# Seven of eight eighths of an MLP's down projection as seven products each, on one NeuronCore

## The chip, the cores and the metric

One core of a Trainium2 chip. The metric is device time in microseconds (us) of one launch. Times of instructions come from one execution that the hardware profiler recorded. PE is TensorE's matmuls, PEld its weight loads, DVE VectorE, ACT ScalarE, POOL GpSimd, SP the engine that issues most transfers.

## What is computed

Two layers of an encoder block on 512 tokens of width 1024, in f32: a mixer (attention and retention), an MLP, and a gated addition. The part that matters here:

```python
u = rms_norm(h, norm_mlp_pre[i])
ff = jnp.square(jax.nn.relu(u @ w_mlp_up[i])) @ w_mlp_down[i]
h = h + rms_norm(ff, norm_mlp_post[i])
gate = jax.nn.sigmoid(rms_norm(h) @ w_ple_gate[i])
h = h + gate * rms_norm(p[i] @ w_ple_proj[i], norm_ple[i])
```

`w_mlp_up` is 1024 x 4096, `w_mlp_down` 4096 x 1024, `w_ple_gate` 1024 x 1024.

## The kernel before, in words

**Matrix products.** Every f32 operand is split into a high part (rounded to fp32r, on ACT) and a low part (the rest, on DVE or POOL). A product of two operands is three matmuls, high x high, high x low and low x high (`HL`, L295). A matmul has a 128 x 128 stationary block and up to 512 moving columns.

**Weights.** They lie in DRAM in the order of use, `PLAN`, as chunks of 512 KB (128 x 1024). `prefetch` (L271) loads a chunk on SP's queue (L254) into one of 4 `raw` buffers, splits it on ACT (L278) and mostly DVE (L301, through `low`) into one of 5 `wt` buffers, up to three items ahead of the one that `chunk` (L289) hands to PE.

**The MLP.** The 4096 inner columns are 32 up chunks. `up_job(c)` (L879) multiplies one (24 matmuls), `evac_up` (L890) applies relu and square. The down projection is cut into eighths of 512 inner rows. The first six (`UNITS`, L56) are done by seven products in place of eight: of a 2 x 2 cut of an eighth (tokens in halves, rows in halves, output columns in halves) `operands` (L826) forms sums of activation blocks on DVE, in a chain in which each of x, y and v needs the one before; `total` (L260) forms the sums of weight blocks by transfers that POOL issues and that add into a buffer (L268); `product` (L843) multiplies (12 matmuls) and `evac_prod` (L855) adds the result to an accumulator `prod` in SBUF (L860). The accumulators of all eighths are folded into the four output quarters once, in the last group: seven additions of 128 x 1024 on DVE (L915), listed in `FOLD`.

The groups are interleaved with the up chunks of the next eighth: up, P1, P5, up, P7, P6, up, P3, P4, up, P2 (L906 to L914). `_slot` (L63) gives the same order to the weights in `PLAN`, and `_items` (L93) to what is converted.

**The plain part.** The last two eighths' activations are kept split (`ff`, L893 to L898); after four more up chunks, `row_job` (L332) runs them as plain products: for each half of the output columns, four weight chunks, 96 matmuls. In the first half each chunk goes over all four token tiles (t); in the second (`ONES`) one tile after another is completed. `h`, which waits in DRAM, is reloaded on SP before (L920) into buffers that the folds free.

**Behind it.** When a tile's second half is complete, `evac_dn` (L929) starts its chain: add to the accumulator (DVE, L933), mean square (ACT, L351), rstd (two small operations on POOL, L359 and L361), gain, residual (DVE, L926), mean square again (ACT), rstd (POOL), `un` (DVE, L403), a transpose of `un` on PE (L413) and the split of the result into `uT` (ACT L416, DVE L417). The gate's matmuls (`pg`) read `uT`. The first half's gain goes on POOL (L935). `un` has two buffers free at this point. A tile's transposes are put into PE's order `AGE_DN` = 6 steps after its end (a step is 6 matmuls in this part), or at the latest by `settle` (L389), in front of the first gate matmul that reads that tile; the gate begins with tiles 0 and 1.

**What sets the order.** PE's order is that of the program text (L206). The other engines' queues are laid out when the program is built, by priority among what is expected to be ready; each then runs in that order. `soon` (L375) raises the priority of an evacuation by 300.

Of the kernel before, what the change touches and what calls it, by code (L numbers as in the profile page):

```python
# [52 lines left out]
ROPE_POOL = ()  # L53
POOL_LOW = ("qa", "ka", "qr", "kr", "vr", "g", "ga", "ao")

UNITS = 6  # L56


def _dn(e, hf, k):
    return 8 * (e // 2) + 4 * hf + 2 * (e % 2) + k  # L60


def _slot(e):  # L63
    up = [("up", 4 * e + 4 + c) for c in range(4)]
    b11, b21, b12, b22 = (("dn", _dn(e, hf, k)) for hf in range(2) for k in range(2))
    return [up[0], b11, b12, up[1], b22, up[2], b21, up[3]]


# [13 lines left out]
    + [("pp", c) for c in range(2)]  # L82
    + [("up", c) for c in range(4)]
    + [x for e in range(UNITS) for x in _slot(e)]
    + [("up", c) for c in range(28, 32)]
    + [("dn", c) for c in range(24, 32)]
    + [("pg", c) for c in range(8)]
)
PLAN = [(i,) + x for i in range(NL) for x in PLAN_LAYER]
CHUNK = {x: n for n, x in enumerate(PLAN)}  # L90


def _items():  # L93
    out = []
    for i in range(NL):
        for kind, c in PLAN_LAYER:
            e = 2 * (c // 8) + c % 4 // 2
            if kind == "up" and c >= 4 and c // 4 <= UNITS:
                e, at = c // 4 - 1, c % 4
                b11, b21, b12, b22 = (CHUNK[i, "dn", _dn(e, hf, k)] for hf in range(2) for k in range(2))  # L100
                out.append(((i, "up", c), (CHUNK[i, "up", c],)))
                out += [((i, p, e), src) for p, src in (
                    (("P1", (b11,)), ("P5", (b11, b12))),
                    (("P7", (b12, b22)), ("P6", ("chain", b22))),
                    (("P3", (b22,)), ("P4", ("chain", b21))),
                    (("P2", (b21,)),),
                )[at]]
            elif kind != "dn" or e >= UNITS:
                out.append(((i, kind, c), (CHUNK[i, kind, c],)))
    return out  # L110


ITEMS = _items()
ITEM = {key: m for m, (key, _) in enumerate(ITEMS)}
LAST = {src[0]: m for m, (_, src) in enumerate(ITEMS) if len(src) == 1}
# [84 lines left out]
def block(ctx: ExitStack, tc: tile.TileContext, x, pT, w, dl, gains, cs, lc, rel, eye, out):  # L200
# [12 lines left out]
    def blk(tag, shape, dt=F32, name="blk"):  # L213
        return big.tile(shape, dt, name=name, tag=tag, bufs=NAMES[tag])
# [7 lines left out]
    def bank(tag):  # L222
        b = banks[tag].pop(0)
        banks[tag].append(b)
        return b
# [63 lines left out]
    def chunk(*key):  # L289
        m = ITEM[key]  # L290
        n = max(x for _, src in ITEMS[max(0, m - 3):m + 4] for x in src if x != "chain")
        prefetch(n + 3, m + 4)
        return wt[m]
# [13 lines left out]
    def t_job(key, ps, rhs=None, kts=KD, off=0):  # L307
        t = chunk(*key)
        for k in range(kts):
            for n, (a, b) in enumerate(HL):  # L310
                r = uT[:, b, k, :] if rhs is None else rhs[k][:, b, :]
                nc.tensor.matmul(ps, lhsT=t[:, a, (off + k) * P:(off + k + 1) * P], rhs=r,  # L312
                                 start=k == 0 and n == 0, stop=k == kts - 1 and n == 2)
            if k % 2:
                step()
# [4 lines left out]
    def row_mm(ps, ch, j, lhs, k, t, first, last):  # L320
        for n, (a, b) in enumerate(HL):
            nc.tensor.matmul(ps, lhsT=lhs(a, k, t), rhs=ch[:, b, j * S:(j + 1) * S],  # L322
                             start=first and n == 0, stop=last and n == 2)

    def step(age=None):
        clock[0] += 1
        age = AGE if age is None else age
        if pending and clock[0] - pending[0][0] >= age:
            soon(pending.pop(0)[1])()
        tick()  # L330

    def row_job(keys, lhs, evac, groups=ALL, age=None):  # L332
        n = len(keys)
        chs = {}
        for grp in groups:
            if lhs is u_lhs:
                settle(grp)
            pss = [bank(ROW_BANKS[n]) for n in range(len(grp))]
            for c in range(len(keys)):
                if grp is groups[0]:  # L340
                    chs[c] = chunk(*keys[c])
                for t, ps in zip(grp, pss):
                    for j in range(2):
                        row_mm(ps, chs[c], j, lhs, 2 * c + j, t, c == 0 and j == 0, c == n - 1 and j == 1)
                    if c == n - 1:
                        evac(t, ps)
                    step(age)
# [41 lines left out]
    def settle(ts):  # L389
        while any(t in unready for t in ts):  # L390
            soon(pending.pop(0)[1])()
# [247 lines left out]
    def one_layer(i, h):  # L639
# [113 lines left out]
        for c in range(8):  # L753
            src = fb[c // 2][:, c % 2, :]
# [44 lines left out]
        def ple_norm(t):  # L799
            junk = blk("R", [P, D], name="pjunk")  # L800
            r = rstd_of(sumsq(pn[t], junk, 4e-6, 1.0 / 16))
            nc.gpsimd.tensor_scalar(pn[t], pn[t], r, 1.0, op0=ALU.mult, op1=ALU.mult)
            nc.gpsimd.tensor_tensor(pn[t], pn[t], g_ple, op=ALU.mult)
# [22 lines left out]
        def operands(f1, f2):  # L826
            a11, a21, a12, a22 = f1[:, :, :256], f1[:, :, 256:], f2[:, :, :256], f2[:, :, 256:]
            ops = {}
            x, y, z, v = (t2(n).rearrange("p (s n) -> p s n", s=2) for n in ("sx", "sy", "sz", "sv"))
            operand(ops, "P1", a11)  # L830
            nc.vector.tensor_tensor(x, a22, a21, op=ALU.subtract)
            operand(ops, "P5", x)
            nc.vector.tensor_tensor(z, a11, a21, op=ALU.subtract)
            operand(ops, "P7", z)
            nc.vector.scalar_tensor_tensor(y, x, -1.0, a11, op0=ALU.mult, op1=ALU.subtract)
            operand(ops, "P6", y)
            nc.vector.scalar_tensor_tensor(v, y, -1.0, a12, op0=ALU.mult, op1=ALU.subtract)
            operand(ops, "P3", v)
            operand(ops, "P4", a22)
            operand(ops, "P2", a12)  # L840
            return ops

        def product(e, x, op):  # L843
            t = chunk(i, x, e)
            for j in range(2):
                ps = dn_bank()
                for k in range(2):
                    for n, (a, b) in enumerate(HL):
                        nc.tensor.matmul(ps, lhsT=op[:, a, k, j * P:(j + 1) * P], rhs=t[:, b, k * S:(k + 1) * S],  # L849
                                         start=k == 0 and n == 0, stop=k == 1 and n == 2)  # L850
                evac_prod(e, x, j, ps)
                step(AGE_DN)
# [26 lines left out]
        def up_job(c):  # L879
            if c < EARLY:  # L880
                ps = early[c]
            else:
                ps = bank("s")
                t_job((i, "up", c), ps)
            if 2 <= c < 6:
                ple_norm(c - 2)
            evac_up(c, ps)

        @soon
        def evac_up(c, ps):  # L890
            r = t2("relu")
            nc.scalar.activation(r, ps, AF.Relu)  # L892
            if c >= 4 * UNITS:  # L893
                b = blk("A", [P, 2, S], F32R, name="ff")
                nc.scalar.activation(b[:, 0, :], r, AF.Square)
                nc.vector.tensor_tensor(r, r, r, op=ALU.mult)
                nc.vector.tensor_tensor(b[:, 1, :], r, b[:, 0, :].bitcast(F32), op=ALU.subtract)
                half_f.append(b)  # L898
                return
            if c % 2 == 0:  # L900
                half_f.append(blk("P", [P, 2, S], name="f"))
            nc.scalar.activation(half_f[-1][:, c % 2, :], r, AF.Square)

        for c in range(4):
            up_job(c)
        for e in range(UNITS):  # L906
            ops = operands(*half_f)
            half_f = []
            for n, xs in enumerate((("P1", "P5"), ("P7", "P6"), ("P3", "P4"), ("P2",))):
                up_job(4 * e + 4 + n)  # L910
                for name in xs:
                    product(e, name, ops[name])
                    if e == UNITS - 1:
                        for to, of in FOLD.get(name, ()):  # L914
                            nc.vector.tensor_tensor(prod[to], prod[to], prod[of], op=ALU.add)  # L915
        for c in range(28, 32):
            up_job(c)
        for t in range(NT):
            h[t] = blk("V", [P, D], name="hr")
            nc.sync.dma_start(h[t], hm[t])  # L920
# [17 lines left out]
            return f  # L938

        for hf in range(2):  # L940
            row_job([(i, "dn", 24 + 4 * hf + c) for c in range(4)],
                    lambda a, k, t: half_f[k][:, a, t * P:(t + 1) * P], evac_dn(hf), ONES if hf else ALL, AGE_DN)

        if not last:
# [20 lines left out]
        if last:  # L965
            t, f = NT - 1, evac_pg(1)
            for j in range(CUTS):
                cut = slice(j * S // CUTS, (j + 1) * S // CUTS)
                n = cut.stop - cut.start
# [67 lines left out]
```

## Time and profile before

| | |
|---|---|
| three runs, median (lowest to highest) | 1794.32 us (1794.28 to 1795.28) |
| the profiled execution, and its span | 1794.64 us, 1792.9 us |
| PE busy | 1772.4 us, 99% of the span |
| DVE, ACT, POOL busy | 64%, 45%, 21% |
| MLP of layer 0, last group of products | 745 to 786 us |
| its four further up chunks | 786 to 808 us |
| its plain part | 808 to 854 us |

The span runs from the first to the last instruction; the execution's own time has some 1.7 us around it. "Busy" counts an engine from an instruction's start to its end, so waits inside the order of work are seen in the idle time that a row gives in brackets, with the instruction or transfer that ended it.

### The profile page before, as it was taken

The page shows a single profiled execution, that of the slowest core. Times are in us where ns is not written, and L with a number is a line of the kernel's source. Part 1 is how long each engine was busy: PE and PEld are TensorE (multiplying, and loading weights), DVE is VectorE, ACT ScalarE, POOL GpSimd, SP SyncE. Part 2 cuts the span into 40 slices and gives each one's busy share as a digit, 9 for nine tenths or more (in the row PEclk, how much of TensorE's full clock was granted, in tenths as well). Part 3 has the DMA queues.
Part 4 walks back from the last instruction along what each step waited for, and adds up shares of the span by engine and source line. Part 5 has one row for each costly group of instructions (what it writes and reads, how often), then busy time and mean ns, then how long its engine had stood idle before and what let it go on. Part 6 is the DMA issues. An engine that isn't in the chain of part 4 may idle for free.

```text
span 1792.9 us, 22127 instructions
## 1 busy us (share of the span) xinstructions
PE 1772.4 (99%) x8209; PEld 1466.2 (82%) x8209; DVE 1145.4 (64%) x1803; ACT 807.5 (45%) x1271; POOL 382.6 (21%) x354
## 2 busy tenths in 40 slices
PE   8999999999999999999999999999999999999998
PEld 6888788888898888888788887888888888888887
DVE  6676777743465677674656767677444657667754
ACT  4255444332466454433443555444333664444342
POOL 2312244311142001002123222442012410000030
PEclk9999999999999999999999999999999999999999
DMA  5555464552347655552346545555422566664421
GB/s 213 194 193 159 149 212 137 166 175 95 117 142 188 165 158 161 156 184 70 129 141 214 165 145 172 184 159 187 136 101 99 165 170 156 169 175 130 165 71 60
DMA packets 87807, 274.58 MB, mean 153 GB/s; under 512 B 11921, under 2 KB 20497, under 8 KB 87698
## 3 DMA queue, kind: packets, MB, share of 16 engines
q1 hardware_dynamic: 80786, 247.99, 40.7%
q0 software_dynamic: 6912, 25.17, 8.3%
q8 instruction: 65, 1.06, 0.2%
q14 instruction: 44, 0.36, 0.1%
HBM read 239.55 MB, written 33.55 MB: 152 GB/s over the span
## 4 chain that ended last, share of the span: by engine, by line
PE 89%; DVE 4%; POOL 2%; ACT 2%; issue 1%; DMA 1%; SPq 0%; POOLq 0%; ACTq 0%
PE acc L312 28%; PE acc L322 19%; PE s L312 18%; PE acc L849 8%; PE tp L849 4%; PE tp L612 2%; PE tp L544 2%; PE tp L507 2%; PE acc L871 1%; PE tp L413 1%; POOL wt L301 1%; PE s L525 1%; PE s L526 1%; PE s L590 1%; PE s L871 1%
## 5 line engine op out<-in xcount | busy, mean ns | idle before, releaser
L312 PE MATMUL acc<-uT,wt 128*128 128x512 f32 x1920 | 472.8, 392 | 0.0
L312 PEld LDWEIGHTS acc<-uT,wt 128*128 128x128 f32 x1920 | 356.2, 188 | 71.8
L301 DVE TENSOR_TENSOR wt<-raw,wt 128x1024 fp32r<-128x1024 f32 x217 | 279.4, 1292 | 187.6 <-ACT wt L278 187.1
L278 ACT ACTIVATE wt<-raw 128x1024 fp32r<-128x1024 f32 x280 | 293.9, 1055 | 223.0 <-PE acc L312 114.0
L322 PE MATMUL acc<-wt,uT 128*128 128x512 f32 x1320 | 320.8, 396 | 4.4 <-ACT uT L416 1.8
L312 PE MATMUL s<-uT,wt 128*128 128x512 f32 x1392 | 323.7, 389 | 0.0
L312 PEld LDWEIGHTS s<-uT,wt 128*128 128x128 f32 x1392 | 261.1, 188 | 54.1
L322 PEld LDWEIGHTS acc<-wt,uT 128*128 128x128 f32 x1320 | 245.6, 189 | 55.6 <-DVE uT L417 2.6
L301 POOL TENSOR_TENSOR wt<-raw,wt 128x512 fp32r<-128x512 f32 x126 | 173.2, 1395 | 408.1 <-ACT wt L278 339.1
L849 PE MATMUL acc<-wt,op 128*128 128x512 f32 x672 | 159.5, 389 | 0.0
L849 PEld LDWEIGHTS acc<-wt,op 128*128 128x128 f32 x672 | 126.1, 188 | 26.2
L268 POOL DMA_DIRECT2D wsum<-in_w_dram x48 | 42.8, 900 | 420.1 <-DVE wt L301 141.0
L892 ACT ACTIVATE relu<-s 128x512 f32<-128x512 f32 x60 | 35.7, 595 | 180.7 <-PE s L312 172.0
L860 DVE TENSOR_TENSOR sumP<-acc,sumP 128x512 f32<-128x512 f32 x92 | 61.8, 686 | 56.4 <-PE acc L849 56.1
L312 PE MATMUL acc<-retT,wt 128*128 128x512 f32 x384 | 89.3, 389 | 0.0
L322 PE MATMUL acc<-wt,ff 128*128 128x512 f32 x384 | 88.5, 390 | 0.0
L301 DVE TENSOR_TENSOR wt<-wsum,wt 128x1024 fp32r<-128x1024 f32 x48 | 60.6, 1263 | 41.7 <-ACT wt L278 41.7
L312 PEld LDWEIGHTS acc<-retT,wt 128*128 128x128 f32 x384 | 72.1, 188 | 15.0
L322 PEld LDWEIGHTS acc<-wt,ff 128*128 128x128 f32 x384 | 71.8, 188 | 14.8
L304 ACT ACTIVATE rt<-rz 128x512 fp32r<-128x512 f32 x64 | 40.3, 631 | 91.5 <-DVE rz L594 91.0
L849 PE MATMUL tp<-wt,op 128*128 128x512 f32 x336 | 80.7, 389 | 0.0
L849 PEld LDWEIGHTS tp<-wt,op 128*128 128x128 f32 x336 | 63.1, 188 | 13.1
(165 smaller groups left out, 2153.5 us busy)
## 6 DMA issues: line engine op xcount, KB each, us to landing
raw<-in_w_dram SPq DMA_DIRECT2D x280, 512.0 KB, 3.7
wsum<-in_w_dram POOLq DMA_DIRECT2D x48, 512.0 KB, 5.5
kk<-stk SPq DMA_DIRECT2D x128, 128.0 KB, 3.8
wsum<-in_w_dram SPq DMA_DIRECT2D x24, 512.0 KB, 3.3
stq<-rr SPq DMA_DIRECT2D x16, 512.0 KB, 3.4
qs<-stq SPq DMA_DIRECT2D x128, 64.0 KB, 2.9
stk<-rr SPq DMA_DIRECT2D x16, 512.0 KB, 3.0
stv<-vr SPq DMA_DIRECT2D x16, 512.0 KB, 4.4
```

The source lines that it names most:

```text
L268: nc.gpsimd.dma_start(r, rows(src[1]), accum_op=ALU.add)
L278: nc.scalar.activation(t[:, 0, :], r, AF.Copy)
L301: eng.tensor_tensor(dst, src, hi.bitcast(F32), op=ALU.subtract)
L304: nc.scalar.activation(dst[:, 0], src, AF.Copy, scale=scale)
L312: nc.tensor.matmul(ps, lhsT=t[:, a, (off + k) * P:(off + k + 1) * P], rhs=r, start=k == 0 and n == 0, stop=k == kts - 1 and n == 2)
L322: nc.tensor.matmul(ps, lhsT=lhs(a, k, t), rhs=ch[:, b, j * S:(j + 1) * S], start=first and n == 0, stop=last and n == 2)
L507: nc.tensor.matmul(o, lhsT=v, rhs=pt[k][:, hl, :], start=k == 0 and hl == 0, stop=k == 3 and hl == 1)
L544: nc.tensor.transpose(ps[:, t * P:(t + 1) * P], zs[t][:, k * P:(k + 1) * P], ident)
L612: nc.tensor.matmul(o, lhsT=v[:, k, a * P:(a + 1) * P], rhs=rt[k][:, b, :], start=n == 0, stop=n == 11)
L849: nc.tensor.matmul(ps, lhsT=op[:, a, k, j * P:(j + 1) * P], rhs=t[:, b, k * S:(k + 1) * S], start=k == 0 and n == 0, stop=k == 1 and n == 2)
L860: nc.vector.tensor_tensor(a, ps, a, op=ALU.add)
L871: nc.tensor.matmul(early[c][:, 256 * j:256 * j + 256], lhsT=t[:, a, k * P:(k + 1) * P], rhs=uT[:, b, k, 256 * j:256 * j + 256], start=k == ...
```

## The change

Seven eighths instead of six go by seven products; one eighth is plain. In the last group the order is P1, P5, up, P7, P6, up, P3, P4, up, P2, up: the products come ahead of the up chunk that they followed, and the folds are in this group. The four up chunks that stood alone between the last group and the plain part are now this group's. A half of the plain part has two weight chunks instead of four.

```diff
-UNITS = 6
+UNITS = 7
...
     b11, b21, b12, b22 = (("dn", _dn(e, hf, k)) for hf in range(2) for k in range(2))
+    if e == UNITS - 1:
+        return [b11, b12, up[0], b22, up[1], b21, up[2], up[3]]
     return [up[0], b11, b12, up[1], b22, up[2], b21, up[3]]
...
     + [x for e in range(UNITS) for x in _slot(e)]
-    + [("up", c) for c in range(28, 32)]
-    + [("dn", c) for c in range(24, 32)]
+    + [("dn", _dn(UNITS, hf, k)) for hf in range(2) for k in range(2)]
...
-                out.append(((i, "up", c), (CHUNK[i, "up", c],)))
-                out += [((i, p, e), src) for p, src in (
+                one = [((i, "up", c), (CHUNK[i, "up", c],))]
+                products = [((i, p, e), src) for p, src in (
...
+                out += products + one if e == UNITS - 1 else one + products
...
-                up_job(4 * e + 4 + n)
+                if e < UNITS - 1:
+                    up_job(4 * e + 4 + n)
                 for name in xs:
                     product(e, name, ops[name])
                     if e == UNITS - 1:
                         for to, of in FOLD.get(name, ()):
                             nc.vector.tensor_tensor(prod[to], prod[to], prod[of], op=ALU.add)
-        for c in range(28, 32):
-            up_job(c)
+                if e == UNITS - 1:
+                    up_job(4 * e + 4 + n)
...
         for hf in range(2):
-            row_job([(i, "dn", 24 + 4 * hf + c) for c in range(4)],
+            row_job([(i, "dn", _dn(UNITS, hf, k)) for k in range(2)],
                     lambda a, k, t: half_f[k][:, a, t * P:(t + 1) * P], evac_dn(hf), ONES if hf else ALL, AGE_DN)
```

## Rows read from the trace of the kernel before

**Rows 1.** the page, parts 1, 2 and 6

```profile
PE 1772.4 (99%) x8209; PEld 1466.2 (82%) x8209; DVE 1145.4 (64%) x1803; ACT 807.5 (45%) x1271; POOL 382.6 (21%) x354
...
PEclk9999999999999999999999999999999999999999
...
raw<-in_w_dram SPq DMA_DIRECT2D x280, 512.0 KB, 3.7
```

**Rows 2.** PE's waits from 40 us to the end: us in total, times, longest

```profile
PE tp L413 <- DVE uT L417: 2.9, 2, 1.5
...
PE tp L413 <- DVE un L403: 0.7, 2, 0.3
```

**Rows 3.** PE's timeline, layer 0: start, us, what, idle before

```profile
742.49 2.88 PE L849 MATMUL acc<-wt,op 128*128 128x512 f32 x12
...
783.29 2.88 PE L849 MATMUL tp<-wt,op 128*128 128x512 f32 x12
786.01 21.92 PE L312 MATMUL s<-uT,wt 128*128 128x512 f32 x96
807.77 34.16 PE L322 MATMUL acc<-wt,ff 128*128 128x512 f32 x150
...
848.70 1.09 PE L413 MATMUL tp<-ident,un 128*128 128x128 f32 x8 [0.34 <-DVE un L403]
...
865.79 1.26 PE L413 MATMUL tp<-ident,un 128*128 128x128 f32 x8 [1.47 <-DVE uT L417]
```

**Rows 4.** groups by line and shape, VectorE, 742.49 to 791.45

```profile
L915 DVE TENSOR_TENSOR sumP<-sumP,sumP 128x1024 f32<-128x1024 f32 x7 | 8.5, 1219 | 0.1
```

**Rows 5.** windows: us; busy PE, PEld, DVE, ACT, POOL; clock; DMA; GB/s

```profile
742.00:767.00 25.00, 25.00 (x112) 20.67 (x112) 17.89 (x25) 12.91 (x19) 0.89 (x1) 1.00 0.46 123
767.00:792.00 25.00, 25.00 (x112) 20.71 (x111) 24.93 (x30) 9.43 (x12) 0.00 (x0) 1.00 0.52 177
```

**Rows 6.** POOL's timeline, layer 0

```profile
758.77 0.89 POOL L268 DMA_DIRECT2D wsum<-in_w_dram  x1 [17.89 <-DVE wt L301]
828.05 6.02 POOL L935 TENSOR_TENSOR sumP<-sumP,gain 128x512 f32<-128x512 f32 x4 [68.40 <-ACT junk L351]
```

**Rows 7.** SP's timeline, layer 0

```profile
791.64 0.33 SPq L920 DMA_DIRECT2D hr<-hm  x1
```

**Rows 8.** VectorE's timeline, the last group's operands

```profile
746.39 0.68 DVE L831 TENSOR_TENSOR sx<-f 128x512 f32<-128x512 f32 x1
...
748.20 0.69 DVE L823 TENSOR_TENSOR op<-sx,op 128x512 fp32r<-128x512 f32 x1
```

**Rows 9.** chain of waits, 820 to 900 us: start, us, what

```profile
835.17 0.70 DVE sumP L933
...
836.70 0.70 POOL rstd L359
...
837.47 0.58 POOL rstd L361
...
838.08 0.76 DVE hr L926
...
839.59 0.73 ACT un L351 x2
...
841.25 0.88 DVE un L403 x2
842.13 0.61 DVE sumP L933
...
854.47 1.65 POOL rstd L361
```

**Rows 10.** VectorE's timeline, last group and tail

```profile
788.59 0.68 DVE L896 TENSOR_TENSOR relu<-relu 128x512 f32<-128x512 f32 x1
...
826.53 1.28 DVE L933 TENSOR_TENSOR sumP<-acc,sumP 128x512 f32<-128x512 f32 x2
...
854.48 1.22 DVE L301 TENSOR_TENSOR wt<-raw,wt 128x1024 fp32r<-128x1024 f32 x1
```

## The prediction

> **What bounds the kernel now.** I read the page first. PE is busy 99% of the span and its granted clock is the upper level (2.4 GHz) in every slice [rows 1], so the time changes by matmuls removed and by PE stalls added or removed. Second, PE's waits after the start [rows 2]: those in the stage that changes are the `uT` transposes (L413), 2.9 us behind VectorE's `uT` and 0.7 us behind VectorE's `un`, each twice, once per layer. Third, PE's timeline of layer 0 [rows 3] puts them in place: 0.34 us ahead of the transposes at 848.70 and 1.47 us ahead of those at 865.79, so 1.81 us per layer. Up and product stretches follow one another without a gap. 96 matmuls take 807.77 - 786.01 = 21.76 us, 0.2267 us each [rows 3]; this pitch is used throughout. An up chunk (24) is 5.44 us, a product (12) 2.72 us.
>
> **The sum is made against the profiled execution**, 1794.64 us with a span of 1792.9 us; the median of the three runs is 0.32 us lower, and the forecast starts from that median.
>
> **Fewer matmuls.** Per layer, the seventh eighth goes from 96 plain matmuls (4 token tiles x 2 halves x 4 blocks x 3) to 7 products of 12 = 84. That is 12 x 0.2267 = **2.72 us less per layer**. No transposes or up matmuls change in number.
>
> **More work beside PE.** The seventh group adds 14 evacuations, 4 sums and 7 operands on VectorE, and needs 9 weight transfers where the plain form had 4. The folds (7 of 1.22 us [rows 4]) stay 7; they move one group later. Is there room? In the last group of before, VectorE is busy 17.89 us of 25, then 24.93 of 25, with no PE stall [rows 5]. In the new order the stretch from P6 on has the same sequence, with up chunks of later numbers. Ahead of P6 the group loses one up chunk: 5.44 us of window, and on VectorE 1.2 us of weight splitting and two operations of 0.68 us of squaring [rows 10], so some 15.3 us of work for 19.6 us. It fits; costed at nothing. If that cover were gone, late evacuations would hold PE by about the excess, one for one.
>
> **Queues.** POOL issues four accumulating transfers more per layer; the last of before's final group is issued at 758.77 [rows 6], 16 us before the P4 that needs it (P2 starts at 783.29 [rows 3], an up chunk and P4 stand in front: 775.13). SP must reload `h` after the folds: the last reload is issued at 791.64 [rows 7], right after the final fold and 5.6 us after the last product. One up chunk now stands between, so this falls 0.2 us behind the start of the plain part; a 512 KB load lands in about 3.7 us [rows 1], and the first reader comes 16.7 us in. Weight loads queued behind it on SP wait with it, but those of the plain part stand in front. Nothing. Likewise chunk 31's evacuation: before, chunk 27's reached VectorE at 788.59 [rows 10], 5.3 us after its matmuls (783.29 [rows 3]), and was the latest; its low part follows 1.2 us later. Chunk 31's is needed 6.1 us into the plain part, its low part 0.45 us after. Nothing, and about 1 us if VectorE is as late again. The second half holds 2 of the 5 `wt` buffers and no longer 4, so two more of the gate's chunks can be split ahead of the tail; no PE wait there names `wt` [rows 2], so this gains nothing either.
>
> **The products in front.** P5 of the last group needs a22 - a21, which needs the last up chunk. Before, an up chunk stood in between. In before that chunk ended at 742.49 [rows 3], the difference was made at 746.39 and the operand's low part at 748.20 to 748.89 [rows 8], 6.40 us after. In the new place P5 starts 5.44 us after, and reads the low part in its third matmul, 5.89 us after: 0.5 us late, or 1.1 with one P1 evacuation newly in front. Laid out anew, the difference may also come sooner, since chunk and evacuation work is in front of it. Ends 0 and 1.1; I take **0.6 us per layer** added, since the nearest row is that very chain.
>
> **The tail of the plain part.** This is the term that decides. A half now has 2 chunks: in the second half, token tiles end 2.72 us apart and not 5.44. Each tile has a chain across engines. For t=0 [rows 9]: subtraction at 835.17, POOL's rstd 836.70, residual 838.08, squares on ScalarE (two of 0.73 us), `un` at 841.25. The tile's matmuls ended at 807.77 + 120 x 0.2267 = 834.97, so the first half of `un` (0.45 us) is there 6.73 us after. The transposes of t=0 come 30 matmuls = 6.80 us after its end, before and after: just in time. Those of t=1 came 7.95 us after its end; now settle asks for them directly behind the second half, 24 matmuls and one set of transposes (0.85 us) after: 6.29 us. Alone it would be 0.44 us late: the lower end of the new stall.
>
> The upper end is the order of before: VectorE takes t=1's subtraction only at 842.13, behind t=0's `un` [rows 9]. Serially, 6.9 us per tile, t=1's first half is ready 13.6 us after t=0's end against 9.01 due, 4.5 us late, and t=3 another 3 us: 7.5 us.
>
> Between them I walked the operations with their durations [rows 9, 10], each engine taking what is ready, earlier tiles first (the first half of before is interleaved so: t=0's and t=1's sums run back to back at 826.53, ahead of the rest of t=0's work [rows 10]). From the start of the plain part: t=0 ends at 13.6, t=1 at 16.3. t=0's `un` comes at 20.95 against 20.4 due, 0.55 us late, having let t=1's subtraction (0.6) in front. t=1's residual halves stand behind t=2's subtraction (0.4) and t=0's `un` (0.8); its second square behind the `uT` copy of t=0 (0.45); its `un` behind a `uT` low part (0.35). It is ready at 24.95 against 22.6: **2.35 us** late in all. t=2 and t=3 have 11 us to their transposes, so both old stalls, 1.81 us, go: t=3's came because `uT` of t=2 was held behind t=3's `un`, which is now long done. POOL's four products of the first half take 6.02 us [rows 6]; moved up by 10.88 us they end at 15.4, just as t=0's rstd wants POOL (15.3).
>
> One more thing adds to 2.35. POOL's power took 1.65 us at 854.47 [rows 9] beside a weight split on VectorE from 854.48 [rows 10], where it takes 0.58 otherwise (837.47): 1.07 us more. In the new order such neighbours are frequent; I add one such wait, and take **3.4 us**. Ends 0.4 and 7.5.
>
> The Trainium skill has a rule that speaks against this change ("SBUF — State Buffer", section "SBUF: two separate sides"): VectorE instructions with two SBUF inputs and GpSimd's instructions take the same port pair exclusively, for a whole instruction. The row at 854.47 agrees with it. By the rule, each of the four POOL operations in t=1's chain could wait for a whole VectorE operation, and the term would be 5.2 us in place of 3.4.
>
> **Sum per layer:** -2.72 - 1.81 + 0.6 + 3.4 = -0.53 us; two layers -1.1 us. 1794.3 - 1.1 = **1793.2 us**, no change that can be told: about 0.2% (3.6 us) is what a measurement of this kernel can tell.
>
> **Rivals.**
> 1. **The chains interleave well** and P5 is in time: -2.72 - 1.81 + 2.35 = -2.18 per layer, 1790.0 us; with the lower end of the stall (0.44) -4.09, 1786.1. For it: the first half of before is interleaved already [rows 10]. Against it: `un` of t=0 was in time by 0.07 us when nothing stood in front. 0.33.
> 2. **Slower: the tail in VectorE's queue.** The order written down at build time keeps whole chains together, as at 842.13. -2.72 - 1.81 + 0.6 + 7.5 = +3.57 per layer, 1801.5 us. It decides as soon as the new stalls pass 5.7 us per layer (then +1.8 each). For it: the row at 842.13, where VectorE idled ahead of `un` while t=1's subtraction was ready at 840.4. Against it: there the two came within 0.8 us; now t=1 is 2.7 us earlier. 0.24.
> 3. **POOL waits in every step**: each of the four in t=1's chain (two for each rstd) held for one VectorE operation of 0.7 us [rows 8]: 2.35 + 2.8 = 5.15 us per layer, so -2.72 - 1.81 + 0.6 + 5.15 = +1.22, and 1796.8 us, still within 0.2%. For it: 854.47. Against it: the other powers and additions of the chain kept their time beside VectorE. The Trainium skill's port rule above would give this time. 0.10.
> 4. **It doesn't do what it says**: matmuls aren't fewer. The loops exclude it; the count below would show it. 0.
>
> **How the numbers follow.** The forecast has 0.33 of its own and rival 3 0.10: both are the same within 0.2%, 0.43 together. Faster 0.33, slower 0.24. The range takes in rival 2's end, 1801.5, and rival 1 down to 1787.5, leaving out its best corner; cases within 0.2% alone would be 1790.7 to 1797.9.
>
> **What would show it.** 24 matmuls fewer. In PE's timeline, the third-matmul stall in the last group's P5 (0 to 1.1 us); a stall of about 3 us in front of the last tiles' transposes, released by VectorE's `un`; none at t=3's. Wrong would be: t=2's subtraction behind t=1's `un` on VectorE (rival 2), a PE stall on evacuations in the last group, or a plain part that waits for chunk 31 or for SP's reloads.

## The result, and the profile after

The changed kernel takes 1809.16 us (median of 5 runs, 1808.27 to 1810.38) where the kernel before takes 1794.32: the ratio is 1.0082, with a 95% interval of 1.007 to 1.0093. It is 14.8 us slower, where 1793.2 us and at most 1801.5 were forecast.

The page of the changed kernel, parts 1 and 2, as [rows 1]:

```profile
PE 1773.4 (98%) x8185; PEld 1466.1 (81%) x8185; DVE 1171.4 (65%) x1843; ACT 821.3 (45%) x1291; POOL 385.8 (21%) x362
...
PEclk9999999999999999999999999999999999999989
```

24 matmuls are gone (8209 to 8185), yet PE is busy 1.0 us longer, and in the last slice but one, the tail of layer 1, the clock is below nine tenths. PE's waits of the changed kernel from 40 us on, as [rows 2] (lines of the kernel are two further down than before):

```profile
PE tp L415 <- DVE ss L355: 12.5, 2, 6.3
...
PE tp L415 <- DVE uT L419: 3.0, 2, 1.5
PE acc L851 <- DVE op L825: 2.0, 2, 1.0
...
PE tp L415 <- DVE un L405: 0.6, 2, 0.3
```

Three of these four are at the transposes. Where before 3.6 us were lost there in all, it is now 16.1. PE's timeline of layer 0 shows the places, as [rows 3]:

```profile
786.42 3.33 PE L851 MATMUL acc<-wt,op 128*128 128x512 f32 x14
790.74 2.60 PE L851 MATMUL acc<-wt,op 128*128 128x512 f32 x10 [0.98 <-DVE op L825]
...
828.54 20.56 PE L324 MATMUL acc<-wt,ff 128*128 128x512 f32 x90
849.40 1.09 PE L415 MATMUL tp<-ident,un 128*128 128x128 f32 x8 [0.30 <-DVE un L405]
850.25 1.63 PE L324 MATMUL acc<-wt,ff 128*128 128x512 f32 x6
858.14 1.11 PE L415 MATMUL tp<-ident,un 128*128 128x128 f32 x4 [6.26 <-DVE ss L355]
860.77 1.11 PE L415 MATMUL tp<-ident,un 128*128 128x128 f32 x4 [1.51 <-DVE uT L419]
861.53 9.38 PE L324 MATMUL acc<-wt,uT 128*128 128x512 f32 x30
870.76 1.04 PE L415 MATMUL tp<-ident,un 128*128 128x128 f32 x8
...
874.38 1.03 PE L415 MATMUL tp<-ident,un 128*128 128x128 f32 x8
```

P5 waits 0.98 us in its third matmul (790.74). The plain part starts at 828.54. The transposes of tile 0 wait 0.30 us, the first four of tile 1 wait 6.26 us, the second four another 1.51. Behind them 30 gate matmuls take 870.76 - 861.53 = 9.23 us; at [rows 3]'s pitch of 0.2267 us they would take 6.80. The windows of that stretch show the granted clock; columns as in [rows 5], the clock is the third number from the right:

```profile
828.50:849.00 20.50, 20.50 (x91) 16.71 (x90) 12.88 (x21) 9.55 (x21) 8.21 (x9) 1.00 0.43 146
...
852.00:858.00 6.00, 0.00 (x0) 0.00 (x0) 4.88 (x9) 4.99 (x11) 2.04 (x4) 0.85 0.27 87
858.00:860.00 2.00, 1.11 (x4) 0.71 (x4) 1.51 (x5) 1.46 (x5) 1.03 (x4) 0.50 0.00 0
...
864.00:866.00 2.00, 2.00 (x7) 1.52 (x6) 1.29 (x2) 0.05 (x1) 1.51 (x2) 0.50 0.18 72
...
868.00:870.00 2.00, 2.00 (x10) 1.66 (x9) 0.00 (x0) 0.00 (x0) 0.00 (x0) 1.00 0.00 0
```

The granted clock is 1.00 up to the wait, 0.85 on average from 852 to 858 us, inside the wait, and 0.50 (the lower of the two levels, 1.2 GHz) from 858 to 866 us. Tile 3's transposes (874.38) no longer wait.

What holds tile 1's transposes is in VectorE's timeline, as [rows 10]:

```profile
848.86 0.88 DVE L405 TENSOR_SCALAR un<-hr,rstd 128x512 f32<-128x512 f32 x2 [1.09 <-POOL rstd L363]
...
852.74 1.23 DVE L303 TENSOR_TENSOR wt<-raw,wt 128x1024 fp32r<-128x1024 f32 x1 [0.41 <-ACT wt L280]
854.68 0.88 DVE L405 TENSOR_SCALAR un<-hr,rstd 128x512 f32<-128x512 f32 x2 [0.71 <-POOL rstd L363]
855.48 0.68 DVE L938 TENSOR_TENSOR sumP<-sumP,gain 128x512 f32<-128x512 f32 x1
856.08 1.40 DVE L929 SCALAR_TENSOR_TENSOR hr<-sumP,rstd,hr 128x512 f32<-128x512 f32 x2
857.40 0.68 DVE L419 TENSOR_TENSOR uT<-tp,uT 128x512 fp32r<-128x512 f32 x1
...
859.23 0.88 DVE L405 TENSOR_SCALAR un<-hr,rstd 128x512 f32<-128x512 f32 x2 [0.49 <-POOL rstd L363]
860.03 0.68 DVE L419 TENSOR_TENSOR uT<-tp,uT 128x512 fp32r<-128x512 f32 x1
```

Tile 1's `un` starts at 854.68, and its first half is there by 855.1. The transposes start at 858.14, when the split of tile 0's first four transposes (L419, 857.40) has ended, and the second four at 860.77, when the split at 860.03 has. The kernel puts transposes into two banks of PSUM, the memory that PE writes to, in turn, four to a bank. These are the tp banks. So tile 1's transposes need the banks that tile 0's are split from; tile 0's were on PE at 849.40. In VectorE's order this split stands behind a weight split (852.74), tile 1's `un`, and tile 2's gain and residual. (The waits view names the small `ss` of VectorE that ended beside the split.)

**The account closes to 0.3 us.** Per layer: -2.72 for the matmuls, -1.81 for the old waits, +0.98 at P5, +8.07 at the transposes, +2.43 for the 30 gate matmuls, and +1.03 for tile 1's eight transposes: from 858.14 to 861.53 without the 1.51 us wait they take 1.88 us, where eight take 0.85. That is 7.98 us, 16.0 us in two layers; the spans differ by 1808.6 - 1792.9 = 15.7. The last term is only in part the clock's. Of the 1.03 us, 0.34 lies in the second four transposes (861.53 - 860.77 = 0.76 us in the place of 0.42). The other 0.69 lies in the first four, ahead of a wait that ends with the split at 860.03 anyway: at full speed the wait would be longer in its place (`e2_fill` below shows it).

### The profile page after: what moved, and what is told of

Read it like the earlier page. It is cut to its first block, busy times and chain, and to the rows that moved or that the text cites. A ratio compares the mean times of both kernels' runs of the same rounds, so it can differ in the third digit from the quotient of the medians.

```text
span 1808.6 us, 22195 instructions
## 1 busy us (share of the span) xinstructions
PE 1773.4 (98%) x8185; PEld 1466.1 (81%) x8185; DVE 1171.4 (65%) x1843; ACT 821.3 (45%) x1291; POOL 385.8 (21%) x362
## 3 DMA queue, kind: packets, MB, share of 16 engines
q8 instruction: 64, 1.05, 0.2%
## 4 chain that ended last, share of the span: by engine, by line
PE 88%; DVE 6%; ACT 2%; POOL 2%; issue 1%; DMA 1%; SPq 0%; ACTq 0%; POOLq 0%
PE acc L314 27%; PE acc L324 18%; PE s L314 17%; PE acc L851 10%; PE tp L851 5%; PE tp L614 2%; PE tp L546 2%; PE tp L509 2%; PE acc L873 1%; PE tp L415 1%; DVE wt L303 1%; POOL wt L303 1%; PE s L527 1%; PE s L528 1%; PE s L873 1%
## 5 line engine op out<-in xcount | busy, mean ns | idle before, releaser
L324 PE MATMUL acc<-wt,uT 128*128 128x512 f32 x1320 | 325.3, 400 | 5.0 <-ACT uT L418 2.2
L851 PE MATMUL acc<-wt,op 128*128 128x512 f32 x792 | 188.6, 389 | 2.0 <-DVE op L825 2.0
L851 PEld LDWEIGHTS acc<-wt,op 128*128 128x128 f32 x792 | 148.4, 188 | 33.7 <-DVE op L825 2.8
L270 POOL DMA_DIRECT2D wsum<-in_w_dram x56 | 49.7, 894 | 487.8 <-DVE sumP L862 133.3
L862 DVE TENSOR_TENSOR sumP<-acc,sumP 128x512 f32<-128x512 f32 x112 | 75.4, 685 | 61.2 <-PE acc L851 60.6
L303 DVE TENSOR_TENSOR wt<-wsum,wt 128x1024 fp32r<-128x1024 f32 x56 | 70.3, 1256 | 47.4 <-ACT wt L280 47.3
L851 PE MATMUL tp<-wt,op 128*128 128x512 f32 x384 | 92.2, 389 | 0.0
L851 PEld LDWEIGHTS tp<-wt,op 128*128 128x128 f32 x384 | 72.1, 188 | 15.0
L280 ACT ACTIVATE wt<-wsum 128x1024 fp32r<-128x1024 f32 x56 | 59.2, 1057 | 53.9 <-DMA wsum<-in_w_dram 32.5
L532 ACT ACTIVATE z<-z,nm 128x512 f32<-128x512 f32 x64 | 46.2, 723 | 56.5 <-DVE nm L531 56.2
```

The lines of the kernel that those rows point to most:

```text
L270: nc.gpsimd.dma_start(r, rows(src[1]), accum_op=ALU.add)
L280: nc.scalar.activation(t[:, 0, :], r, AF.Copy)
L303: eng.tensor_tensor(dst, src, hi.bitcast(F32), op=ALU.subtract)
L532: nc.scalar.activation(z, z, AF.Exp, bias=nm, scale=-1.0, accum_out=den)
L862: nc.vector.tensor_tensor(a, ps, a, op=ALU.add)
```

## The experiments

The theory after the result: tiles are completed too close together ahead of the gate; VectorE's queue then holds `un`, and still longer the split that frees the tp banks; and PE's wait costs clock on top. Against it: the seventh group itself, or its products in front, overload VectorE. All ratios are to the kernel before, with 95% intervals; medians in us.

**Each part alone.** `e3_tail_alone` is the kernel before with another order in the second half of the plain part only:

```diff
+        for t, c in [(t, c) for c in range(2) for t in range(4)] + [(t, c) for t in range(4) for c in (2, 3)]:
...
+            if c == 3:
+                f1(t, pss[t])
```

> The kernel before (six eighths by products, 192 plain matmuls), with only the order of the second half of the plain part changed: its first two weight chunks go over all four tiles, and then each tile is completed with the other two, so that tiles are completed 2.72 us apart as in the change. If the tail is what costs, the stalls of the change appear (8 us in the place of 1.8, and the low clock): 6 to 9 us per layer, 1806 to 1812 us. If the seventh group or the products in front cost, the time stays: 1794 us.

Measured: 1813.03, ratio 1.0103 (1.0086 to 1.0119). PE's timeline of this kernel, layer 0:

```profile
859.60 1.12 PE L413 MATMUL tp<-ident,un 128*128 128x128 f32 x4 [6.25 <-DVE ss L353]
862.23 1.11 PE L413 MATMUL tp<-ident,un 128*128 128x128 f32 x4 [1.51 <-DVE uT L417]
863.00 8.61 PE L322 MATMUL acc<-wt,uT 128*128 128x512 f32 x30
871.45 1.04 PE L413 MATMUL tp<-ident,un 128*128 128x128 f32 x8
```

The same 6.25 and 1.51 us, and 8.45 us for the 30 matmuls behind them, with not one product more than before. The tail alone gives the whole loss: some 18 us. That is the change's 14.8, plus the 5.4 us of matmuls that the change saves, less the 2.0 us that it loses at P5.

`e4_front_alone` puts the last group's products in front in the kernel before, with the `_slot`, `_items` and loop edits of the change and `UNITS` left at 6.

> The kernel before with only the last group's products put in front of its up chunks (six eighths by products, the four further up chunks and the plain part as before). If the products in front cost only P5's wait for its operand, 1.0 us per layer: 1796 us. If they are the main cost of the change: over 1800 us.

Measured: 1796.75, ratio 1.0014 (1.0005 to 1.0023). Its only new PE wait is P5's, 0.96 us in layer 0. `e8_up_first` undoes the same move in the changed kernel.

> The changed kernel with the last group in the order of the other groups (up, P1, P5, up, P7, P6, ...): the move of the products to the front undone, the seventh group kept. The wait at P5 (1.0 us per layer) goes; the last evacuated activations then come 2.7 us sooner against the plain part and the folds later. If the move costs only P5's wait: 1807 us. If the folds behind the last product hold the plain part: 1809 us or more.

Measured: 1806.68, ratio 1.007 (1.0055 to 1.0085), 2.5 us under the change; P5's wait is gone, the waits at the transposes are as in the change. So the move costs what its wait costs, in either kernel, and the folds hold nothing.

**What holds tile 1's transposes.** `e1_s_banks`: the changed kernel with another pair of banks for odd tiles.

```diff
-                ps = bank("tp")
+                ps = bank(tag)
...
+                    pre_norm(h[t], t, None, upd_mlp(t, rstd_of(*ssq[t])), "s" if t % 2 else "tp")
```

> The changed kernel, with the transposes of tiles 1 and 3 behind the plain part going to the two s banks of PSUM, which are idle there, and those of tiles 0 and 2 to the two tp banks as before. If the tp banks are what holds tile 1's transposes (its un is there about 855.1, the transposes start at 858.1 and 860.8), they start 3 us sooner, the second wait of 1.5 us goes, and 3 to 4.5 us per layer come back: 1800 to 1803 us. If VectorE's chain of un alone holds them, nothing moves: 1809 us.

Measured: 1804.7, ratio 1.0053 (1.0038 to 1.0068). PE's timeline, layer 0:

```profile
855.15 1.36 PE L415 MATMUL s<-ident,un 128*128 128x128 f32 x8 [3.34 <-DVE un L405]
...
858.07 2.93 PE L324 MATMUL acc<-wt,uT 128*128 128x512 f32 x6 [0.70 <-DVE ss L355]
862.56 6.92 PE L324 MATMUL acc<-wt,uT 128*128 128x512 f32 x22 [1.56 <-DVE uT L419]
```

Without the bank, tile 1's transposes go when `un` is there (855.15, 3.34 us late). That is the term the prediction had. But the gate's matmuls now wait for the splits themselves (0.70 and 1.56 us), and less comes back than expected. `e7_split_first` leaves the banks and changes the order of VectorE and ScalarE, in the tail of the plain part only:

```diff
-            soon(pending.pop(0)[1])()
+            soon(*pending.pop(0)[1])()
...
-        pending.append((clock[0], rest))
+        pending.append((clock[0], (rest, 2 * PRIO if gain is None else PRIO)))
```

> The changed kernel with the split of a tile's transposes into uT raised in priority behind the plain part, so that VectorE and ScalarE do tile 0's split ahead of tile 1's un and tile 2's residual, and nothing else in their order. If the order of VectorE's queue (the split standing 3 us behind other tiles' steps, with the tp banks held so long) is the larger part of the stall, tile 1's transposes start with its un, now 1.2 us later than 855, the wait between its two sets of transposes goes, and 2 to 4 us per layer come back: 1801 to 1805 us. If un alone decides, VectorE has the same work in front of it and the time stays: 1808 to 1810 us.

Measured: 1798.87, ratio 1.0029 (1.0018 to 1.0041): 10.3 us under the change, more than expected. PE's timeline, layer 0, and a window behind it:

```profile
853.86 1.59 PE L415 MATMUL tp<-ident,un 128*128 128x128 f32 x8 [3.86 <-DVE un L405]
```

```profile
856.00:858.00 2.00, 2.00 (x6) 1.51 (x6) 2.00 (x5) 0.75 (x3) 0.00 (x0) 0.57 0.00 0
```

Tile 1's transposes have one wait of 3.86 us, for `un`, and none for a bank. So of the 8.07 us, 3.6 (e1, with tile 0's 0.30) to 4.2 (e7, with tile 0's 0.29) are `un`, and the rest is the order in which VectorE splits.

**The clock.** `e2_fill` puts 24 matmuls that nobody reads into the wait of the changed kernel (`nc.tensor.matmul(wps, lhsT=half_f[0][:, 0, :P], rhs=half_f[0][:, 0, :], ...)`).

> The changed kernel with 24 matmuls of 512 columns, whose result nobody reads, between the plain part and tile 1's transposes: 5.4 us of PE work in the place of the 6.3 us wait, so the stall that counts stays and PE isn't idle. If the granted clock of 0.50 behind that wait (858 to 866 us) comes from the idle PE, it stays at 1.00, the 30 gate matmuls take 6.8 us in the place of 9.2, and the time falls by 2.5 to 3 us per layer: 1803 to 1804 us. If those matmuls are slow for another reason (late uT, weights), the time stays: 1809 us.

Measured: 1807.82, ratio 1.0072 (1.0057 to 1.0087). The windows of this kernel:

```profile
856.00:858.00 2.00, 2.00 (x10) 1.66 (x9) 1.81 (x4) 1.36 (x2) 1.03 (x3) 1.00 0.73 236
...
860.00:862.00 2.00, 0.31 (x3) 0.07 (x1) 1.51 (x4) 1.21 (x3) 1.40 (x4) 1.00 0.00 0
...
864.00:866.00 2.00, 2.00 (x6) 1.56 (x5) 1.51 (x5) 0.97 (x4) 0.74 (x2) 0.50 0.73 242
866.00:868.00 2.00, 2.00 (x9) 1.60 (x9) 1.92 (x3) 0.00 (x0) 0.00 (x0) 0.95 0.03 10
```

The clock stays at 1.00 through the filled wait, but two more waits, 0.81 and 1.97 us around four transposes, are left behind it, and then it is 0.50: the test is not clean. PE's timeline at the second of them:

```profile
862.28 0.68 PE L415 MATMUL tp<-ident,un 128*128 128x128 f32 x4 [1.97 <-DVE uT L419]
```

The first four transposes start at 859.66, 2.62 us before these, and at a clock of 1.00; in the change it is 2.63 us at 0.50. So the low clock cost nothing between the two sets. The four executions follow the mean granted clock: 1805.56 and 1805.81 us at 0.999, 1809.83 and 1810.31 at 0.997, the traced one among the latter. Filling the wait did pay where the clock stayed up. `e10_split_fill` repeats it in e7, which has one wait only, with 17 matmuls.

> The kernel of e7 with 17 matmuls of 512 columns, whose result nobody reads, in the place of the 3.9 us wait ahead of tile 1's transposes. If the low clock behind the wait (0.57 from 854 to 858 us) comes from the idle PE, it stays at 1.00, the 30 gate matmuls take 6.8 us in the place of 8.1, and 1.3 us per layer come back: 1796 us. If it comes from something else (the transposes, the turn to the gate), the time stays: 1799 us.

Measured: 1798.32, ratio 1.0022 (1.0013 to 1.0031), no better than e7 by what can be told. The windows (852 to 862) and PE's timeline:

```profile
854.00:856.00 2.00, 1.97 (x12) 1.40 (x11) 1.95 (x5) 1.54 (x3) 1.04 (x4) 1.00 0.65 193
...
858.00:860.00 2.00, 1.11 (x4) 0.63 (x5) 1.99 (x4) 2.00 (x7) 0.00 (x0) 1.00 0.00 0
```

```profile
855.46 1.09 PE L415 MATMUL tp<-ident,un 128*128 128x128 f32 x8
856.31 1.64 PE L324 MATMUL acc<-wt,uT 128*128 128x512 f32 x6
858.89 6.03 PE L324 MATMUL acc<-wt,uT 128*128 128x512 f32 x24 [0.94 <-ACT uT L418]
```

The clock is 1.00 throughout, so the idle wait is what lowered it in e7 (0.57 there from 854 to 858 us). But PE now waits 0.94 us for tile 1's split, where e7 has no wait. ScalarE's timelines, of e7 and then of this kernel, show where it comes from:

```profile
854.63 0.60 ACT L418 ACTIVATE uT<-tp 128x512 fp32r<-128x512 f32 x1 [0.69 <-PE tp L415]
```

```profile
857.63 0.63 ACT L353 ACTIVATE un<-hr 128x512 f32<-128x512 f32 x1 [2.08 <-DVE hr L929]
...
858.26 1.06 ACT L418 ACTIVATE uT<-tp 128x512 fp32r<-128x512 f32 x2
```

In e7 the first half of the split starts on ScalarE 0.77 us after tile 1's transposes. Here it starts 2.80 us after them, behind a square of tile 2 that ScalarE idles 2.08 us for. The added matmuls changed the order of the queues as well as the clock. So this run shows what lowers the clock, but its unchanged time doesn't show what the low clock costs.

**A version that spreads the tiles.** `e5_spread` changes the order inside the plain part of the changed kernel (and the order of its four weight chunks to match):

```diff
+        for t, hf, c in ([(t, hf, 0) for hf in range(2) for t in (0, 1)] + [(t, hf, 1) for t in (0, 1) for hf in range(2)]
+                         + [(t, hf, c) for t in (2, 3) for hf in range(2) for c in range(2)]):
```

> The changed kernel with only the order inside the plain part changed: the first weight chunk of both halves goes over tiles 0 and 1, then tile 0 is completed, tile 1, tile 2 and tile 3, each in both halves, so that they are complete 8.2, 10.9, 16.3 and 21.8 us into the part (before: 13.6, 16.3, 19.0, 21.8). Matmuls are as many as in the change. If tiles completed too close before the gate are the cause, the stall of 8 us per layer and the low clock go, down to 0 to 2 us: 1787 to 1792 us, faster than before the change. If the seventh group is too much for VectorE, it stays over 1800 us.

Measured: 1795.31, ratio 1.0005 (0.9996 to 1.0015), between the two expectations. 13.9 us of the loss are gone with the same matmuls and the same seventh group, but 0.46 and 2.36 us of waiting for `un` are left, and the clock falls behind the second. `e6_spread_p5` adds the order P1, up, P5, P7, up, P6, P3, up, P4, P2, up in the last group.

> The kernel of e5 with another order in the last group: P1, up, P5, P7, up, P6, P3, up, P4, P2, up. P5 comes one up chunk later, so its wait for the operand (1.0 us per layer) should go: 2 us under e5. The group's additions move against the up chunks; if VectorE is late with chunk 31 or the folds, up to 2 us come back and it equals e5.

Measured: 1791.97, ratio 0.9988 (0.9978 to 0.9997). P5's wait is gone.

`e9_spread_later` raises the age of the transposes by 2 steps in the plain part of e6 (`step(AGE_DN + 2)`).

> The kernel of e6 with the transposes of a tile of the plain part put into PE's order 8 steps after the tile's end in the place of 6. In e6 PE waits 0.46 and 2.35 us per layer for un ahead of the transposes of tiles 0 and 1, and the granted clock is 0.50 for some 3 us behind the second wait. Two steps are 2.7 us: both waits go, and if the low clock comes from the wait, it stays at 1.00, another 1 to 2 us per layer: 1783 to 1786 us. If only the waits go and the clock falls anyway: 1786 to 1788 us.

Measured: 1796.37, ratio 1.0011 (1.0003 to 1.002): a miss. `un` is no longer waited for, but tile 1's transposes wait 4.15 and 0.38 us in layer 0. `e12_spread_gain` takes POOL's products away from e6 (`nc.vector.tensor_tensor(a, a, g_mpost...)` for both halves).

> The kernel of e6 with the first half's gain multiplied on VectorE in the place of POOL. In e5 un took 1.85 to 1.90 us (two operations) beside POOL's products, where it takes 0.88 otherwise. If POOL's products hold VectorE there, un takes 0.9 us, the wait ahead of tile 1's transposes (2.35 us) falls by 1 us or more, for 0.6 us of VectorE work more per tile: 1789 to 1791 us. If un is slow for another reason, the added work makes it 1792 us or more.

Measured: 1794.99, ratio 1.0005 (0.9996 to 1.0014). VectorE's timeline of e5, and then of this kernel:

```profile
841.75 1.90 DVE L405 TENSOR_SCALAR un<-hr,rstd 128x512 f32<-128x512 f32 x2 [1.03 <-POOL rstd L363]
```

```profile
839.37 0.88 DVE L403 TENSOR_SCALAR un<-hr,rstd 128x512 f32<-128x512 f32 x2 [1.03 <-POOL rstd L361]
```

`un` takes 0.88 us where it took 1.90 beside POOL's product (POOL: 841.68 for 1.29 us in e5). That half of the expectation holds; the time does not, since tile 1 now waits 1.58 us for `un` and 1.61 us for the split.

**Banks, order or `un`.** Three more runs settle what e9 left open. `e13_spread_banks` is e9 with the s banks of e1, `e15_spread_first` is e9 with the priority of e7, and `e14_spread_all` has both.

> The kernel of e9 (spread plain part, P5 one up chunk later, transposes 8 steps after a tile's end) with tiles 1 and 3 transposed into the s banks, as in e1. In e9 PE waited 4.15 and 0.38 us per layer ahead of tile 1's two sets of transposes. If these were waits for the tp banks, which tile 0's split on VectorE frees, they go; what is left is the split itself, needed by the gate's first matmuls. With no wait left the granted clock stays at 1.00 and the kernel is what the sum of the prediction gives with no new stall: 1794.4 - 2 x (2.72 + 1.81) = 1785.3 us, up to 1789 us if the gate waits for a split. If un was late there as well, 2 to 4 us per layer stay: 1792 to 1796 us.

Measured: 1798.63, ratio 1.0023 (1.0014 to 1.0033), above every time expected and no faster than e9, whose interval overlaps. The waits at the transposes fall to 0.35 us, so in e9 they were for banks. But the gate now waits for the splits, 3.8 us in layer 0, and 0.77 us for a weight split.

> The kernel of e9 with the split raised in priority, and the two tp banks as before. If e9's waits are for banks that the split frees, the order alone does what the s banks do in e13: 1785 to 1790 us. If un is what is late: 1792 us or more.

Measured: 1790.75, ratio 0.9981 (0.9972 to 0.999), just above the range expected for banks. Tile 1's transposes still wait 2.01 us per layer for the split, so the order alone doesn't free the tp banks in time.

> The kernel of e13 with the split of the transposes raised in priority as in e7. If VectorE's order still holds a split where PE needs it, this is 1 to 4 us under e13, down to 1785 us; if raising the split only pushes un back, as in e11, it is 1 to 3 us over e13.

Measured: 1790.19, ratio 0.9978 (0.9969 to 0.9987). PE's waits of this kernel that are left from 40 us on, without the mixer's:

```profile
PE acc L322 <- DVE uT L417: 2.2, 2, 1.1
...
PE acc L322 <- DVE wt L301: 1.4, 2, 0.7
...
PE s L413 <- DVE un L403: 0.7, 2, 0.4
PE acc L322 <- ACT uT L416: 0.6, 2, 0.3
```

The granted clock is 1.0 over the whole span. 4.9 us of waits in all are left. The prediction's first two terms alone (fewer matmuls, no old waits) give 1794.3 - 9.1 = 1785.2 us, and with 4.9 that is 1790.1. This closes the account from the other side: no other loss of the seventh group shows. Its median is the lowest here (e15 can't be told from it), below both the change and the kernel before.

Last, `e11_before_split_first`: the priority of e7 in the kernel before.

> The kernel before, with only the split of a tile's transposes raised in priority behind the plain part, as in e7. If the wait of 1.47 us per layer at tile 3's transposes came from the order of VectorE's queue (the split of tile 2 behind tile 3's un), it goes: 1791 to 1792 us. If tile 3's chain itself is that late, it stays: 1794 us.

Measured: 1795.34, ratio 1.0008 (0.9999 to 1.0016): no gain. The wait for the split at tile 3 is gone, but tile 1 now waits 1.59 us and tile 3 1.11 us for `un`, which the split pushes back. In the kernel before, the order of VectorE's queue only chooses where PE waits.

## Why the prediction was wrong

**Fewer matmuls, the old waits, queues, cover.** Right: 24 fewer, 1.81 us of old waits gone, tile 3's transposes in time. SP's reloads, POOL's transfers, chunk 31 and VectorE's load in the last group hold PE nowhere: between 770 and 830 us its one wait is P5's.

**The products in front.** Taken at 0.6 us per layer (0 to 1.1), measured 0.98.

**The tail: this step failed, as a sum that left two terms out.** The term that it had, `un` of tile 1, was there, and about as large as forecast: the step put its stall at 3.4 us, and in e1, where `un` is what the transposes wait for, it is 3.34 and 0.30, and in e7, which splits in the order of the walk, 3.86 and 0.29. That it came so close was in part luck. Tile 0's wait was taken at 0.55 and measured 0.30. The 1.07 us for POOL's power was not there; in its place ScalarE copied a weight chunk (851.67, 1.04 us) between tile 1's two squares (851.04 and 852.62), and an addition of POOL took 0.62 us (853.40), 0.43 more than its usual 0.19.

The first term left out is the split. The walk ended when `un` was ready; it let tile 0's split run beside it (0.35 us) and never asked what tile 1's transposes write into. The walk let earlier tiles go first, but the program issues tile 0's split only 6 steps after that tile's end, behind tile 2's evacuation, and in VectorE's order the steps of tiles 1 and 2 stand ahead of it. The wait became 8.07 us, above the upper end of 7.5. The prediction had the evidence: the 1.47 us at 865.79 [rows 3] was a wait for a split, and it was read as a relic that would go.

The second term left out is the clock. The text took the pitch of 0.2267 us throughout, though it forecast a wait longer than any in the trace of before. Behind the wait the clock was 0.50, and the slow matmuls and transposes in the rows above took 2.43 + 0.34 us per layer more than at the pitch. No run gives just this back: e2 left waits, e10 changed the queues. The Trainium skill names this in "TensorE: Matmul & The Clock Gate", section "Why this matters for your kernels": keep idle gaps out of matmul work, or the clock goes back to half. The trace agrees (0.50 at 858 to 866 us), and the prediction has no term for it.

**Rival 2, slower in VectorE's queue,** was the right side, but as a chain of `un` whole behind `un`. VectorE did interleave the tiles: tile 1's subtraction and tile 2's stand between. The queue decided by the place of the split. **Rival 3, the port.** "SBUF — State Buffer", section "SBUF: two separate sides", in the Trainium skill, also has VectorE's faster two-port mode among what POOL holds up; e5 and e12 agree with it (`un` 1.90 beside POOL's product, 0.88 without). In the changed kernel's tail POOL's powers took 0.55 to 0.72 us, and the one slow addition of tile 1's chain is 0.43 us of 8.07, so it was not what decided.

## What to carry to other kernels

When work is taken from PE ahead of a stage that consumes results tile by tile, reckon the chain through to the buffer that PE writes next: here the split that empties a PSUM bank, not the operand, was last. Spread the completion of tiles over the matmuls that are left, and set the priority of the step that frees a bank together with it; either alone left a wait (2.36 us in e5, 3.86 in e7). A forecast wait on PE longer than any in the trace needs a term for the clock behind it.

## What was not expected of the hardware

The granted clock went to 0.50 behind waits of 6.26 us (the change, 858 to 866), and to about 0.5 to 0.57 behind 3.86 (e7) and behind 2.36 us (e5); behind 1.47 us in the kernel before it did not [rows 3], and with the wait filled by matmuls (e10) neither. It was back at 1.00 by 868 us in the change and by 858 us in e7, with PE at work in between.

The length of the wait alone doesn't settle it. In e15 tile 1's transposes wait 2.01 us in both layers; these are the windows behind the wait, in layer 0 and in layer 1:

```profile
850.00:852.00 2.00, 2.00 (x9) 1.71 (x8) 2.00 (x5) 1.83 (x5) 0.00 (x0) 0.50 0.04 8
```

```profile
1734.00:1736.00 2.00, 1.76 (x11) 1.48 (x12) 2.00 (x4) 0.70 (x2) 0.26 (x1) 1.00 0.00 0
```

The clock fell in one and stayed up in the other. So it was in e13: the same three waits (0.84, 1.05 and 1.88 us in layer 0) left it at 1.00 in layer 0 and took it to 0.80 and 0.77 in layer 1 (1744 to 1752 us). What decides this, these runs don't show.
